# Values of a gated recurrence: products for three heads at a time instead of two

## The chip, the cores and the metric

The kernel runs on one core of a Trainium2 chip. The metric is the time of one execution on the device in microseconds (us). Engines are called as the profile calls them: PE (TensorE, matrix products), DVE (VectorE), ACT (ScalarE), POOL (GpSimd) and SP (SyncE, which here issues most of the DMAs). Matrix products are written to PSUM, in banks of 512 float32 columns; everything else lies in SBUF with 128 partitions.

## The reference

One layer of a decoder on 1024 positions of width 1024: a token mixer with residual, then an MLP with squared ReLU and residual, then a final norm. The mixer makes one projection of the normed input and cuts it into a pooling part (256 columns) and four parts of 768 columns for six heads of a gated linear recurrence. What matters here is where the values `v` come from and who reads them:

```python
h = rms_norm(x, norm_mix_g[l])
u = h @ w_in[l]
u_pool, q_raw, f_raw, i_raw, g_raw = jnp.split(u, splits, axis=-1)
...
k = (1.0 - lbf) * jax.nn.sigmoid(-z)          # z = f_raw; forget f = lb + (1-lb) sigmoid(z)
q = jax.nn.silu(q_raw.astype(jnp.float32))
v = i_raw.astype(jnp.float32)
...
o = (jnp.einsum('bhts,bhsv->bhtv', scores, vb)
     + jnp.einsum('bhtk,bhkv->bhtv', qb * jnp.exp(b), state))
new_state = (jnp.exp(b_last[:, :, 0, :])[..., None] * state
             + jnp.einsum('bhsk,bhsv->bhkv', kb * jnp.exp(b_last - b), vb))
```

Each head has 128 columns of values, so `v` is the product of h (1024 x 1024) with 768 columns of `w_in`, 128 for each head. The outputs of the heads are normed, gated with `silu(g_raw)`, joined with the pooling part and multiplied with `w_out`.

## The kernel before

**Products.** A float32 product is made of three reduced ones: each operand is split into a high part (a cast on ACT) and a low part (a subtraction on DVE), `split` at line 116, and `mm3` at line 121 adds high x high, high x low and low x high. The input lies transposed in `hT`: two halves of 512 positions, each with 8 k-tiles (KT = 8). The row scale of the RMS norm is applied after the products (`rms_col`, `rms_row`, from `row_scales`, line 286).

Queries, forget gates and output gates of a head are "dense_T" products (line 347): 128 columns of weights stand in the array and 512 positions stream through. Each has two halves of 8 steps, and a step is one `mm3` of 512 columns. Values are made the other way round, with positions as the stationary side and weight columns streaming, two heads (a pair, 256 columns) at a time.

**Weights** come through two rings: `raw`, two places for what a DMA brings, and `whi`/`wlo`, four places each for the split parts (`load_w`, line 156). A place is taken again when all readers of its former tile are done. A pair's value weights are two tiles of 4 k-tiles each (`v_weights`, line 214). Values of a head lie in a tile `V`, a ring of three buffers (line 315).

**The start** (lines 643 to 723) has the order of PE, DVE and ACT written out by hand. x arrives k-tile by k-tile with the value weights of the first pair in between; `first_V` (line 268) makes the products of a half of the positions, 96 matmuls, while they arrive. Then come the first halves of q and f of head 0, the second half of x, the second half of the values, the second halves of q and f.

**The heads** (lines 725 to 741) have PE's order written out by hand, while DVE, ACT and POOL are ordered by a planner. A head (`hgrn`, line 394) is a chain of stages, `near`, `middle`, `far`, `keys`, `updates`, `output`; each stage ends in PE work that needs DVE's and ACT's work of the stage before. In front of each stage, PE does a set number of steps of other work, `beside(hd)` (line 602): the q, f and gate products of the next heads and the values of the next pairs. `LAGS` (line 34) holds these numbers: with 48 steps beside a head (the first and the last) 5, 14, 8, 4, 1, 9; with 64 steps 6, 19, 10, 4, 1, 10; head 0 gets 9 more before `near` (`FIRST_LAG`). What is left of `beside` is done after the last stage. Half of a pair's values is made at the end of heads 1 and 3, the other half at the start of heads 2 and 4 (`half_V`, line 595).

The stage `near` starts with two products of q and k, q times the decay, one combining step on q and k (lines 399 to 406, all on DVE) and two copies on ACT (lines 411 and 412); k and the decay come from `forget` (line 365): eviction of the product (line 356, DVE), two sigmoids and a scaling on ACT (368 to 370), and on POOL the decay (371).

After the mixer come `w_out`, the norm, and the MLP, which the change does not touch.

Of the kernel before, what the change touches and what calls it, by code (L numbers as in the profile page):

```python
# [10 lines left out]
F32 = mybir.dt.float32  # L11
F32R = mybir.dt.float32r
# [5 lines left out]
P = 128  # L18
S = 1024
# [13 lines left out]
STAGES = ("near", "middle", "far", "keys", "updates", "output")  # L33
LAGS = {48: dict(zip(STAGES, (5, 14, 8, 4, 1, 9))), 64: dict(zip(STAGES, (6, 19, 10, 4, 1, 10)))}
FIRST_LAG = 9
WARM_UP = 8
MIX_ORDER = (2, 3, 4, 5, 6, 0, 1, 7)
LEVELS = (1, 2, 4, 8, 16, 32)

FIRST_ORDER = (1, 2, 5, 6, 3, 7, 4)  # L40
# [22 lines left out]
def kernel(  # L63
# [116 lines left out]
    with ExitStack() as pa:  # L180
# [32 lines left out]

        def v_weights(pair):
            c0 = V0 + pair * 256
            return [load_w(w_in_v[:, 4 * b:4 * b + 4, c0:c0 + 256], [4, 256], f"v{pair}_{b}") for b in range(2)]

        warm = small.tile([P, 1], F32, tag="ss", name="warm")
        act.activation(warm, nhalf[:, :1], AF.Square)
        act.dma_start(g1, norm_mix_g)  # L220
        act.dma_start(lbl, hgrn_lb_logits)

# [44 lines left out]

        def first_V(h, ws):


            banks = [misc_ps(f"ps_v0_{h}_{i}") for i in range(2)]
            for j in range(KT):
                (wh, wl), b = ws[j // 4], j % 4
                for parts in (((0, wh), (0, wl)), ((1, wh),)):
                    for i in range(4):
                        for part, w in parts:
                            pe.matmul(
                                banks[i // 2][:, i % 2 * 256:(i % 2 + 1) * 256],
                                hT[h][part][:, j, i * P:(i + 1) * P], w[:, b, :],
                                start=j == 0 and i % 2 == 0 and part == 0 and w is wh,  # L280
                                stop=j == KT - 1 and part == 1, skip_group_check=i % 2 == 1,
                            )
                yield
            return banks

        def row_scales(h, tiles):

            ss = small.tile([P, 4], F32, tag="sso", name=f"ssx_{h}")
            for i, t in enumerate(tiles):
                squares = ha.tile([P, D], BF16, tag="pair", name=f"squares_{h}_{i}", bufs=3)  # L290
                act.activation(squares, t, AF.Square, accum_out=ss[:, i:i + 1])
# [4 lines left out]
            pool.tensor_tensor(out=r, in0=ms, in1=nhalf[:, :4], op=ALU.pow)  # L296
# [3 lines left out]
            pt = misc_ps(f"pt_rms_{h}")  # L300
# [11 lines left out]

        def values(pair):
            for hd in (2 * pair, 2 * pair + 1):
                vts[hd] = ha.tile([P, NT, P], F32, tag="V", name=f"V_{hd}", bufs=3)

        def dense_V(pair, ws, i):

            if i == 0:
                values(pair)  # L320
            ps = dense_ps(f"ps_v{pair}_{i}")
            for e in range(2):
                h, c = hT[(i + e) // 4], ((i + e) % 4) * P
                for j in range(KT):
                    w = ws[j // 4]
                    mm3(
                        ps[:, e * 256:(e + 1) * 256],
                        (h[0][:, j, c:c + P], h[1][:, j, c:c + P]),
                        (w[0][:, j % 4, :], w[1][:, j % 4, :]),
                        j == 0, j == KT - 1,  # L330
                    )
                    if j % 2:
                        yield
            return ps

        def scaled_V(pair, ps, i):
            for hd in range(2):
                for e in range(2):
                    act.activation(
                        vts[2 * pair + hd][:, i + e, :], ps[:, e * 256 + hd * P:e * 256 + (hd + 1) * P],  # L340
                        AF.Copy, scale=rms_col[:, i + e:i + e + 1],
                    )

# [233 lines left out]
        def pool_output(kt, u):  # L577
            t = ha.tile([P, S], F32, tag="V", name=f"mix_{kt}", bufs=3)
# [15 lines left out]

        def half_V(pair, half):
            if half == 0:
                pair_w[pair] = v_weights(pair)
            for i in (4 * half, 4 * half + 2):
                ps = yield from dense_V(pair, pair_w[pair], i)
                scaled_V(pair, ps, i)  # L600

        def beside(hd):

            if hd in (2, 4):
                yield from half_V(hd // 2, 1)
            if hd + 1 < NH:
# [7 lines left out]
            if hd + 2 < NH:  # L614
                yield from gate(hd)
            elif hd + 1 < NH:
                pooled[0] = yield from pool_input(0, [mix_tile(NH - 1, f"win{n}_0") for n in range(2)])
            else:
# [8 lines left out]
                yield from work  # L627
            if hd in (1, 3):
                yield from half_V((hd + 1) // 2, 0)

        heads, gates, pair_w, pooled, ready_w, xts, w0 = {}, {}, {}, {}, {}, {}, []

# [10 lines left out]
        with tc.manual_schedule(engines={mybir.EngineType.PE, mybir.EngineType.DVE, mybir.EngineType.Activation}):  # L643
            for j in load_xt(0, (("Q", 2), ("Q", 2), ("K", 2), ("K", 2))):
                xt_hi(0, j)
                if j % 4 == 0:
                    raw = wraw.tile([P, 4, 256], F32, tag="raw", name=f"raw_v0_{j // 4}")
                    w0.append([wring["split"][0].tile([P, 4, 256], F32R, tag=f"w{part}", name=f"w{part}_v0_{j // 4}") for part in ("hi", "lo")])

                n = 1 if j < 2 else 2 if j % 2 == 0 else 0  # L650
                if n:
                    ks = slice(j % 4, j % 4 + n)
                    nc.sync.dma_start(raw[:, ks], w_in_v[:, j:j + n, V0:V0 + 256])
# [5 lines left out]
            xns += [load_rows(i) for i in range(2, 4)]  # L659
            for _ in load_xt(1, (("F", 1), ("V", 3), ("G", 1), ("S", 1))):  # L660
                pass
            xns += [load_rows(i) for i in range(4, NT)]
            split(*later.pop(0))

# [17 lines left out]
            steps(scales, 3)  # L682
            vps = finish(first_V(0, w0))
            work_q, work_f = gated(q, wq, 0, "q_0"), forget(f, k, wf, 0, 0)
            steps(work_q)
            steps(work_f)
            for j in range(KT):
                xt_hi(1, j)
                xt_lo(1, j)
                if j % 2 and j < 4:  # L690
                    scaled_V(0, vps[j // 2], j - 1)
                elif j == 5:
                    finish(scales)
            vps = finish(first_V(1, w0))
            finish(work_q)
            finish(work_f)

# [6 lines left out]
            act.copy(dmask, mraw[:, 2 * len(LEVELS), :])  # L704
            scales = row_scales(1, xns[4:])
            steps(scales, 5)
            for e, ps in enumerate(vps):
                scaled_V(0, ps, 4 + 2 * e)
            ready_w["q"] = q_weights(1)
            work_q = gated(q, wq, 1, "q_0")  # L710
            steps(work_q)
            finish(scales)
            finish(work_q)
# [604 lines left out]
```

## Time and profile before

| | |
|---|---|
| time, median of 3 runs | 1074.33 us (1074.18 to 1074.35) |
| the profiled execution | 1074.34 us, of which 1072.4 us from its first to its last instruction (the span) |
| granted clock of PE | 0.998 |
| PE busy from 4.8 to 29.5 us, the start | 24.33 of 24.70 us |
| PE, DVE, ACT busy from 61.9 to 364.9 us, the six heads | 303.0, 195.9, 150.6 of 303.0 us |
| first product of values | 4.81 us |
| first `near` product of heads 0 to 5 | 61.9, 98.9, 153.7, 208.1, 262.9, 316.6 us |

A line of the chain of waits gives a start, a duration and what ran; "x96" means that so many pieces were merged. A line of the timeline has start, duration, engine, source line, operation, what it writes and reads, and shape; in brackets stands how long the engine sat idle before it and what ended that. A line of a group of instructions ends with busy time, mean of one in ns, and idle time before them with the releaser. Busy times of matmuls overlap; their pace is read from their starts. The rows of stretches (from:to) give length, then busy time and number of instructions for PE, PEld, DVE, ACT and POOL, granted clock, DMA share and GB/s.

### The profile page before, as it was taken

The page shows a single profiled execution, that of the slowest core. Times are in us where ns is not written, and L with a number is a line of the kernel's source. Part 1 is how long each engine was busy: PE and PEld are TensorE (multiplying, and loading weights), DVE is VectorE, ACT ScalarE, POOL GpSimd, SP SyncE. Part 2 cuts the span into 40 slices and gives each one's busy share as a digit, 9 for nine tenths or more (in the row PEclk, how much of TensorE's full clock was granted, in tenths as well). Part 3 has the DMA queues.
Part 4 walks back from the last instruction along what each step waited for, and adds up shares of the span by engine and source line. Part 5 has one row for each costly group of instructions (what it writes and reads, how often), then busy time and mean ns, then how long its engine had stood idle before and what let it go on. Part 6 is the DMA issues. An engine that isn't in the chain of part 4 may idle for free.

```text
span 1072.4 us, 14951 instructions
## 1 busy us (share of the span) xinstructions
PE 1063.8 (99%) x6118; PEld 892.3 (83%) x6118; DVE 740.8 (69%) x922; ACT 446.6 (42%) x716; POOL 79.9 (7%) x125
## 2 busy tenths in 40 slices
PE   9999999999999999999999999999999999999997
PEld 7978898889888788888888888888888888888886
DVE  5488735764576823799856855876879878677775
ACT  7765444554434622473223223323425242423334
POOL 1010000100010111101001101100100000000001
PEclk9999999999999999999999999999999999999999
DMA  9421102110210444135434534428993244254104
GB/s 325 141 77 40 41 21 60 40 41 21 60 40 21 134 142 137 69 108 177 156 116 179 184 100 168 177 96 307 380 348 125 101 174 163 112 197 156 40 1 157
DMA packets 71540, 137.59 MB, mean 128 GB/s; under 512 B 5040, under 2 KB 45104, under 8 KB 67888
## 3 DMA queue, kind: packets, MB, share of 16 engines
q1 hardware_dynamic: 60688, 100.97, 27.8%
q0 software_dynamic: 9344, 33.56, 8.1%
q10 hardware_dynamic: 1440, 2.10, 0.5%
q8 instruction: 48, 0.79, 0.3%
q14 instruction: 20, 0.16, 0.1%
HBM read 98.87 MB, written 37.75 MB: 127 GB/s over the span
## 4 chain that ended last, share of the span: by engine, by line
PE 98%; DMA 0%; DVE 0%; ACT 0%; SPq 0%; issue 0%; POOL 0%; ACTq 0%
PE ps_ua L126 5%; PE ps_ua L125 5%; PE ps_ua L124 5%; PE ps_dx L124 5%; PE ps_dx L125 5%; PE ps_dx L126 5%; PE ps_o L126 3%; PE ps_o L124 3%; PE ps_o L125 3%; PE ps_uc L126 3%; PE ps_dy L124 3%; PE ps_uc L125 3%; PE ps_dy L125 3%; PE ps_dy L126 3%; PE ps_uc L124 3%; PE ps_f L124 2%
## 5 line engine op out<-in xcount | busy, mean ns | idle before, releaser
L118 ACT CAST wdop<-raw_wd 128x2048 fp32r<-128x2048 f32 x28 | 53.6, 1913 | 154.6 <-PE ps_dy L126 49.6
L124 PE MATMUL ps_ua<-h2op,whi_wu 128*128 128x512 f32 x256 | 99.8, 390 | 0.0
L126 PE MATMUL ps_ua<-h2op,wlo_wu 128*128 128x512 f32 x256 | 99.7, 389 | 0.0
L125 PE MATMUL ps_ua<-h2op,whi_wu 128*128 128x512 f32 x256 | 99.7, 389 | 0.0
L126 PE MATMUL ps_dx<-wdop,hop 128*128 128x512 f32 x252 | 98.1, 389 | 0.0
L124 PE MATMUL ps_dx<-wdop,hop 128*128 128x512 f32 x252 | 98.1, 389 | 0.0
L125 PE MATMUL ps_dx<-wdop,hop 128*128 128x512 f32 x252 | 98.1, 389 | 0.0
L119 DVE TENSOR_TENSOR wdop<-raw_wd,wdop 128x2048 fp32r<-128x2048 f32 x28 | 64.1, 2290 | 27.7 <-ACT wdop L118 27.7
L118 ACT CAST hop<-hraw 128x2048 fp32r<-128x2048 f32 x28 | 53.4, 1910 | 33.2 <-DMA hraw<-hid 21.4
L119 DVE TENSOR_TENSOR hop<-hraw,hop 128x2048 fp32r<-128x2048 f32 x28 | 64.0, 2284 | 3.0 <-ACT hop L118 3.0
L118 ACT CAST whi_wu<-wsum 128x1024 fp32r<-128x1024 f32 x22 | 23.2, 1054 | 93.2 <-PE ps_ub L126 27.5
L119 DVE TENSOR_TENSOR wlo_wu<-raw_wu,whi_wu 128x1024 fp32r<-128x1024 f32 x23 | 28.0, 1222 | 47.5 <-ACT whi_wu L118 47.5
L801 DVE TENSOR_TENSOR x<-ps_dx,x 128x512 f32<-128x512 f32 x64 | 43.9, 688 | 18.7 <-PE ps_dx L126 18.7
L125 PEld LDWEIGHTS ps_ua<-h2op,whi_wu 128*128 128x128 f32 x256 | 48.1, 188 | 10.0
L124 PEld LDWEIGHTS ps_ua<-h2op,whi_wu 128*128 128x128 f32 x256 | 48.1, 188 | 10.0
L126 PEld LDWEIGHTS ps_ua<-h2op,wlo_wu 128*128 128x128 f32 x256 | 48.1, 188 | 9.9
L126 PEld LDWEIGHTS ps_dx<-wdop,hop 128*128 128x128 f32 x252 | 47.3, 188 | 9.9
L124 PEld LDWEIGHTS ps_dx<-wdop,hop 128*128 128x128 f32 x252 | 47.3, 188 | 9.8
L125 PEld LDWEIGHTS ps_dx<-wdop,hop 128*128 128x128 f32 x252 | 47.3, 188 | 9.7
L1034 POOL DMA_DIRECT2D hid<-hid x56 | 29.8, 532 | 283.5 <-DVE hid L1031 216.5
L126 PE MATMUL ps_uc<-h2op,wlo_wu 128*128 128x512 f32 x128 | 49.8, 389 | 0.0
L125 PE MATMUL ps_dy<-wdop,hop 128*128 128x512 f32 x128 | 49.8, 389 | 0.0
(271 smaller groups left out, 2771.2 us busy)
## 6 DMA issues: line engine op xcount, KB each, us to landing
hid<-hid POOLq DMA_DIRECT2D x56, 512.0 KB, 3.3
hraw<-hid SPq DMA_DIRECT2D x28, 1024.0 KB, 5.3
raw_wu<-in_w_up_dram SPq DMA_DIRECT2D x32, 512.0 KB, 3.7
raw_wd<-in_w_down_dram SPq DMA_DIRECT2D x16, 1024.0 KB, 7.2
xt<-in_x_t_dram SPq DMA_DIRECT2D x16, 256.0 KB, 5.9
xn<-in_x_dram SPq DMA_DIRECT2D x8, 512.0 KB, 7.5
x<-x_mid SPq DMA_DIRECT2D x8, 512.0 KB, 5.6
raw_q<-in_w_in_dram SPq DMA_DIRECT2D x6, 512.0 KB, 4.0
```

Source lines behind the costliest of these rows:

```text
L118: act.copy(hi, src)
L119: dve.tensor_tensor(out=lo, in0=src, in1=hi.bitcast(F32), op=ALU.subtract)
L124: pe.matmul(ps, lh, rh, start=start, stop=False, skip_group_check=goes_on)
L125: pe.matmul(ps, lh, rl, start=False, stop=False, skip_group_check=goes_on)
L126: pe.matmul(ps, ll, rh, start=False, stop=stop, skip_group_check=goes_on)
L801: dve.tensor_tensor(out=out_, in0=a, in1=b, op=ALU.add)
L1034: nc.gpsimd.dma_start(store[n][:, at, :], t)
```

## The change

Values are made for three heads (384 columns) in one product instead of two (256). There are two trios in place of three pairs:

- The first trio is made ahead of all else: both halves of `first_V`, then everything of q and f of head 0. Four banks hold four row tiles of 384 columns each, three of them from the dense pool (first half) or the misc pool (second half), one from the score pool.
- The second trio is made beside head 2 (`TRIO - 1`), at the start of its side work, 8 row tiles of 8 steps; a step is one `mm3` of 384 columns. Gate 2 is made at the start of the side work of head 3.
- A trio's weights are four tiles of 2 k-tiles each, so they fill the split ring.
- The ring of values has four buffers.
- Heads 1 and 4 have 48 steps beside them and take the lags of 48; head 2 has 96 and a new row of lags; head 3 has 64.
- At the start, all of the second half of x is loaded before any rows, the logits' DMA moves from ACT's queue to SP's behind the first four rows of x, and the second half of x is cast before the norm's squares.

```diff
-LAGS = {48: dict(zip(STAGES, (5, 14, 8, 4, 1, 9))), 64: dict(zip(STAGES, (6, 19, 10, 4, 1, 10)))}
+LAGS = {48: (5, 14, 8, 4, 1, 9), 64: (6, 19, 10, 4, 1, 10), 96: (8, 26, 14, 7, 2, 14)}
+LAGS = {steps: dict(zip(STAGES, lags)) for steps, lags in LAGS.items()}
...
+TRIO = 3
...
-        def v_weights(pair):
-            c0 = V0 + pair * 256
-            return [load_w(w_in_v[:, 4 * b:4 * b + 4, c0:c0 + 256], [4, 256], f"v{pair}_{b}") for b in range(2)]
+        VC = TRIO * P
+
+        def v_weights(trio):
+            c0 = V0 + trio * VC
+            return [load_w(w_in_v[:, 2 * b:2 * b + 2, c0:c0 + VC], [2, VC], f"v{trio}_{b}") for b in range(KT // 2)]
...
-        act.dma_start(lbl, hgrn_lb_logits)
...
-        def first_V(h, ws):
-
-
-            banks = [misc_ps(f"ps_v0_{h}_{i}") for i in range(2)]
+        def first_V(h, ws, place):
+
+
+            banks = [(score_ps if i == 3 else place)(f"ps_v0_{h}_{i}") for i in range(4)]
             for j in range(KT):
-                (wh, wl), b = ws[j // 4], j % 4
+                (wh, wl), b = ws[j // 2], j % 2
                 for parts in (((0, wh), (0, wl)), ((1, wh),)):
                     for i in range(4):
                         for part, w in parts:
                             pe.matmul(
-                                banks[i // 2][:, i % 2 * 256:(i % 2 + 1) * 256],
-                                hT[h][part][:, j, i * P:(i + 1) * P], w[:, b, :],
-                                start=j == 0 and i % 2 == 0 and part == 0 and w is wh,
-                                stop=j == KT - 1 and part == 1, skip_group_check=i % 2 == 1,
+                                banks[i][:, :VC], hT[h][part][:, j, i * P:(i + 1) * P], w[:, b, :],
+                                start=j == 0 and part == 0 and w is wh, stop=j == KT - 1 and part == 1,
                             )
...
+        def values(trio):
+            for hd in range(TRIO * trio, TRIO * (trio + 1)):
+                vts[hd] = ha.tile([P, NT, P], F32, tag="V", name=f"V_{hd}", bufs=4)
+
+        def dense_V(trio):
+
+            ws = v_weights(trio)
+            values(trio)
+            for i in range(NT):
+                h, c = hT[i // 4], i % 4 * P
+                ps = dense_ps(f"ps_v{trio}_{i}")
                 for j in range(KT):
-                    w = ws[j // 4]
+                    w = ws[j // 2]
                     mm3(
-                        ps[:, e * 256:(e + 1) * 256],
-                        (h[0][:, j, c:c + P], h[1][:, j, c:c + P]),
-                        (w[0][:, j % 4, :], w[1][:, j % 4, :]),
+                        ps[:, :VC], (h[0][:, j, c:c + P], h[1][:, j, c:c + P]), (w[0][:, j % 2, :], w[1][:, j % 2, :]),
                         j == 0, j == KT - 1,
                     )
-                    if j % 2:
-                        yield
-            return ps
+                    yield
+                scaled_V(trio, ps, i)
...
         def beside(hd):
 
-            if hd in (2, 4):
-                yield from half_V(hd // 2, 1)
+            if hd == TRIO - 1:
+                yield from dense_V(1)
+            elif hd == TRIO:
+                yield from gate(hd - 1)
...
             if hd + 2 < NH:
-                yield from gate(hd)
+                if hd != TRIO - 1:
+                    yield from gate(hd)
...
-            if hd in (1, 3):
-                yield from half_V((hd + 1) // 2, 0)
...
-                if j % 4 == 0:
-                    raw = wraw.tile([P, 4, 256], F32, tag="raw", name=f"raw_v0_{j // 4}")
...
+                if j % 2 == 0:
+                    raw = wraw.tile([P, 2, VC], F32, tag="raw", name=f"raw_v0_{j // 2}")
...
+            for _ in load_xt(1, (("F", 1), ("V", 4), ("G", 1), ("S", 1))):
+                pass
+            xns = [load_rows(i) for i in range(4)]
+            nc.sync.dma_start(lbl, hgrn_lb_logits)
             wq = q_weights(0, early_raw("T", "q_0"), put_off)
-            xns = [load_rows(i) for i in range(2)]
             wf = f_weights(0, early_raw("Kn", "f0"), put_off)
...
+            vps = finish(first_V(0, w0, dense_ps))
+            for j in range(KT):
+                xt_hi(1, j)
+                xt_lo(1, j)
...
-            scales = row_scales(0, xns[:4])
-            steps(scales, 2)
+            scales = [row_scales(0, xns[:4], dense_ps), row_scales(1, xns[4:])]
+            steps(scales[0], 5)
             split(*later.pop(0))
...
+            for i, ps in enumerate(vps):
+                scaled_V(0, ps, i)
+            vps = finish(first_V(1, w0, misc_ps))
+            split(*later.pop(0))
+            steps(scales[1], 5)
+            finish(scales[0])
+            for i, ps in enumerate(vps):
+                scaled_V(0, ps, 4 + i)
...
             ready_w["q"] = q_weights(1)
-            work_q = gated(q, wq, 1, "q_0")
-            steps(work_q)
-            finish(scales)
-            finish(work_q)
+            finish(gated(q, wq, 0, "q_0"))
             ready_w["f"] = f_weights(1)
+            finish(forget(f, k, wf, 0, 0))
+            finish(scales[1])
+            finish(gated(q, wq, 1, "q_0"))
             finish(forget(f, k, wf, 1, 0))
...
-                lags = LAGS[64 if 0 < hd < NH - 1 else 48]
+                lags = LAGS[{TRIO - 1: 96, TRIO: 64}.get(hd, 48)]
```

More of the change, by code (lines that the diff above doesn't have):

```diff
@@ L284, in first_V, with row_scales @@
             return banks
-        def row_scales(h, tiles):
+        def row_scales(h, tiles, place=misc_ps):
             ss = small.tile([P, 4], F32, tag="sso", name=f"ssx_{h}")
@@ L299, in row_scales @@
             yield
-            pt = misc_ps(f"pt_rms_{h}")
+            pt = place(f"pt_rms_{h}")
             for i in range(4):
@@ L311, in finish, with scaled_V @@
                     return end.value
[L313 to L323, printed above, removed]
+        def values(trio):
[7 more added lines that the diff above has]
+                ps = dense_ps(f"ps_v{trio}_{i}")
                 for j in range(KT):
-                    w = ws[j // 4]
+                    w = ws[j // 2]
                     mm3(
-                        ps[:, e * 256:(e + 1) * 256],
-                        (h[0][:, j, c:c + P], h[1][:, j, c:c + P]),
-                        (w[0][:, j % 4, :], w[1][:, j % 4, :]),
+                        ps[:, :VC], (h[0][:, j, c:c + P], h[1][:, j, c:c + P]), (w[0][:, j % 2, :], w[1][:, j % 2, :]),
                         j == 0, j == KT - 1,
                     )
-                    if j % 2:
-                        yield
-            return ps
[L336 to L342, printed above, removed]
+                    yield
+                scaled_V(trio, ps, i)
+        def scaled_V(trio, ps, i):
+            for n in range(TRIO):
+                act.activation(
+                    vts[TRIO * trio + n][:, i, :], ps[:, n * P:(n + 1) * P], AF.Copy, scale=rms_col[:, i:i + 1]
+                )
         def col_tile(c0, name, raw=None, parts=split):
@@ L577, in pool_output @@
         def pool_output(kt, u):
-            t = ha.tile([P, S], F32, tag="V", name=f"mix_{kt}", bufs=3)
+            t = ha.tile([P, S], F32, tag="V", name=f"mix_{kt}", bufs=4)
             for b in range(2):
@@ L593, in gate @@
                 yield from gated(g, wg, h, f"g_{hd}")
[L595 to L600, printed above, removed]
         def beside(hd):
-            if hd in (2, 4):
-                yield from half_V(hd // 2, 1)
+            if hd == TRIO - 1:
+                yield from dense_V(1)
+            elif hd == TRIO:
+                yield from gate(hd - 1)
             if hd + 1 < NH:
@@ L627, in beside @@
                 yield from work
-            if hd in (1, 3):
-                yield from half_V((hd + 1) // 2, 0)
-        heads, gates, pair_w, pooled, ready_w, xts, w0 = {}, {}, {}, {}, {}, {}, []
+        heads, gates, pooled, ready_w, xts, w0 = {}, {}, {}, {}, {}, []
         def steps(work, n=KT):
@@ L645 @@
                 xt_hi(0, j)
-                if j % 4 == 0:
-                    raw = wraw.tile([P, 4, 256], F32, tag="raw", name=f"raw_v0_{j // 4}")
-                    w0.append([wring["split"][0].tile([P, 4, 256], F32R, tag=f"w{part}", name=f"w{part}_v0_{j // 4}") for part in ("hi", "lo")])
+                if j % 2 == 0:
+                    raw = wraw.tile([P, 2, VC], F32, tag="raw", name=f"raw_v0_{j // 2}")
+                    w0.append([wring["split"][0].tile([P, 2, VC], F32R, tag=f"w{part}", name=f"w{part}_v0_{j // 2}") for part in ("hi", "lo")])
                 n = 1 if j < 2 else 2 if j % 2 == 0 else 0
                 if n:
-                    ks = slice(j % 4, j % 4 + n)
-                    nc.sync.dma_start(raw[:, ks], w_in_v[:, j:j + n, V0:V0 + 256])
+                    ks = slice(j % 2, j % 2 + n)
+                    nc.sync.dma_start(raw[:, ks], w_in_v[:, j:j + n, V0:V0 + VC])
                     split(w0[-1][0][:, ks], w0[-1][1][:, ks], raw[:, ks])
                 xt_lo(0, j)
+            for _ in load_xt(1, (("F", 1), ("V", 4), ("G", 1), ("S", 1))):
+                pass
+            xns = [load_rows(i) for i in range(4)]
+            nc.sync.dma_start(lbl, hgrn_lb_logits)
             wq = q_weights(0, early_raw("T", "q_0"), put_off)
-            xns = [load_rows(i) for i in range(2)]
             wf = f_weights(0, early_raw("Kn", "f0"), put_off)
-            xns += [load_rows(i) for i in range(2, 4)]
-            for _ in load_xt(1, (("F", 1), ("V", 3), ("G", 1), ("S", 1))):
-                pass
             xns += [load_rows(i) for i in range(4, NT)]
-            split(*later.pop(0))
+            vps = finish(first_V(0, w0, dense_ps))
+            for j in range(KT):
+                xt_hi(1, j)
+                xt_lo(1, j)
             mx = small.tile([P, NH], F32, tag="lbt", name="lb_shift")
@@ L678 @@
             values(0)
-            scales = row_scales(0, xns[:4])
-            steps(scales, 2)
+            scales = [row_scales(0, xns[:4], dense_ps), row_scales(1, xns[4:])]
+            steps(scales[0], 5)
             split(*later.pop(0))
-            steps(scales, 3)
-            vps = finish(first_V(0, w0))
-            work_q, work_f = gated(q, wq, 0, "q_0"), forget(f, k, wf, 0, 0)
-            steps(work_q)
[L686 to L692, printed above, removed]
-                    finish(scales)
-            vps = finish(first_V(1, w0))
-            finish(work_q)
-            finish(work_f)
+            for i, ps in enumerate(vps):
[6 more added lines that the diff above has]
+                scaled_V(0, ps, 4 + i)
             pool.memset(ones, 1.0)
```

7 lines of the change are left out of this document (removed).

## The prediction

> **What bounds the kernel now.** I read the page first (busy shares and rate of loading), then TensorE's list of waits, then the chain of waits.
>
> ```profile
> span 1072.4 us, 14951 instructions
> PE 1063.8 (99%) x6118; PEld 892.3 (83%) x6118; DVE 740.8 (69%) x922; ACT 446.6 (42%) x716; POOL 79.9 (7%) x125
> ...
> GB/s 325 141 77 40 41 21 60 40 41 21 60 40 21 134 142 137 69 108 177 156 116 179 184 100 168 177 96 307 380 348 125 101 174 163 112 197 156 40 1 157
> ```
>
> ```profile
> PE warm L225 <- DVE junk L223: 1.2, 1, 1.2
> PE ps_v L277 <- DVE wlo_v L119: 0.3, 1, 0.3
> ```
>
> TensorE (PE) is busy for 99% of the span, and its waits in all are 1.5 us, both at the start. In the six heads it never waits. So an edit counts in two ways only: by how much time the matmuls take end to end, and by any wait that it puts in front of TensorE. Work on VectorE (DVE), ScalarE (ACT) or the queues is free until it makes TensorE wait.
>
> What does a matmul cost in a stream? Busy times overlap, so I take starts from the chain: 96 products of 256 columns in one piece, and, from a stretch of the MLP, 24 products of 512 columns between two starts.
>
> ```profile
> 29.53 11.51 PE ps_v L277 x96
> ```
>
> ```profile
> 504.97 0.23 PE ps_ua L124
> ...
> 510.41 0.23 PE ps_uc L124
> ```
>
> 11.51/96 = 119.9 ns for 256 columns; 5.44/24 = 226.7 ns for 512. The difference is 106.8 ns for 256 columns, or 0.417 ns a column, which leaves 13.1 ns that every matmul pays whatever its width. For 384 columns, an estimate by the same line: 13.1 + 160.2 = 173.3 ns.
>
> **Part 1: fewer, wider products.** Before, values take 3 pairs x 8 row tiles x 8 k-tiles x 3 terms = 576 matmuls of 256 columns, 576 x 0.1199 = 69.06 us. After, 2 trios x 8 x 8 x 3 = 384 of 384 columns, 66.55 us. The saving is 192 fixed shares of 13.1 ns, 2.5 us.
>
> [...]
>
> **Part 2: the start.** The first value weights arrive with the first x tiles, and now each k-tile brings half as many bytes again.
>
> ```profile
> 3.05 4.93 DMA raw_v<-in_w_in_dram
> 8.00 0.63 ACT whi_v L118
> 8.65 0.70 DVE wlo_v L119
> 9.40 8.79 PE ps_v L277 x71
> ```
>
> ```profile
> 52.69 1.05 ACT L118 CAST whi_g<-raw_g 128x1024 fp32r<-128x1024 f32 x1 [2.01 <-DMA raw_g<-in_w_in_dram]
> ```
>
> ```profile
> 53.77 1.22 DVE L119 TENSOR_TENSOR wlo_g<-raw_g,whi_g 128x1024 fp32r<-128x1024 f32 x1 [0.60 <-ACT whi_g L118]
> ```
>
> Today the weights of k-tiles 2 and 3 land at 7.98 us; after a cast and a subtraction TensorE starts the second product of k-tile 2 at 9.40, and 71 of the half's 96 products remain. The 25 products before that hide inside the loading. After, 262 KB more have to land by then (half of 524 KB); at the page's 325 GB/s that is 0.8 us. The two splits work on 768 instead of 512 columns: between 0.63 and 1.05 for the cast, so 0.84; between 0.70 and 1.22 for the subtraction, so 0.96. So 9.40 becomes 9.40 + 0.8 + 0.21 + 0.26, about 10.6 us. From there it is matmuls alone: before 9.40 + (71 + 96 + 384) x 0.1199 = 75.5; after 10.6 + (71 + 96 + 192) x 0.1733 = 72.8. **Parts 1 and 2 together: -2.6 us.** Bounds: the 25 wider products take 4.33 us themselves, and they start at about 4.9, so 9.8 is the earliest with a few at the slow pace of the start (-3.4); weights another 0.8 us late give -1.8.
>
> What else is moved at the start. The raw ring has two places, so the weights of k-tiles 4-5 and 6-7 are issued on SP only after the split of tiles 0-1 and 2-3, and x tiles 5 to 7, the second half of x, all rows, the logits (which leave ACT's queue for SP's) and the raw q and f stand behind them on SP. A k-tile now occupies TensorE for 12 x 0.1733 = 2.1 us, so k-tile 6 is needed at about 18.8 us; its weights, issued at 10.6 and in transit for the 4.93 us of the row above, are split by about 17.3. All four places of the split ring hold first-trio weights; the split of q therefore waits on ACT until TensorE has done k-tile 1 of the second half, and the scaling of the values and the other squares queue behind it. The cover is the second half itself, 96 x 0.1733 = 16.6 us.
>
> ```profile
> L339 ACT ACTIVATE V<-ps_v,rms_col 128x128 f32<-128x128 f32 x48 | 14.2, 372 | 17.1 <-PE ps_v L126 15.4 <-POOL rms_col L296 1.5
> L291 ACT ACTIVATE squares<-xn 128x1024 bf16<-128x1024 f32 x8 | 8.4, 1047 | 0.4 <-DMA xn<-in_x_dram 0.2
> ```
>
> ACT has 8 squares (8.4), 12 scalings (at most 12 x 0.37 = 4.4) and two casts (2.1) to do there, 14.9 us. They begin when the logits land, behind 7.9 MB, which at 325 GB/s is some 25 us from the start, and end at about 40; the first result of TensorE that needs them, the row scales for the first q product, is due at about 45 (10.6 + 167 x 0.1733 + 24 x 0.2267). I cost it at nothing; without that cover it would be up to 3 us.
>
> **Part 3: the third head, where a wait appears.** Work beside head 2 now ends with the forget product of head 3, because gate 2 has moved to the front of head 3's own side work. The first scores of head 3 ("near") follow only 6 steps later. What they need is a chain: evict the forget product, two sigmoids and a scaling on ACT (the decay factor is made on POOL beside them), then five passes on DVE, then two copies on ACT. Head 0 shows this chain in today's trace, since there too the forget product comes last, but with 14 steps (5 + 9) in front. First TensorE, then DVE, then ACT:
>
> ```profile
> 52.28 0.39 PE L124 MATMUL ps_q<-hT_hi,whi_q 128*128 128x512 f32 x1
> ```
>
> ```profile
> 52.48 0.69 DVE L356 TENSOR_TENSOR K<-ps_f,rms_row 128x512 f32<-128x512 f32 x1 [0.54 <-PE ps_f L126]
> ...
> 55.73 1.23 DVE L399 TENSOR_TENSOR d<-Q,K 128x1024 f32<-128x1024 f32 x1 [0.74 <-ACT K L370]
> 57.06 1.23 DVE L400 TENSOR_TENSOR Q<-Q,F 128x1024 f32<-128x1024 f32 x1
> 58.21 1.22 DVE L119 TENSOR_TENSOR wlo_q<-raw_q,whi_q 128x1024 fp32r<-128x1024 f32 x1
> 59.34 0.69 DVE L402 TENSOR_TENSOR d<-Q,K 128x512 f32<-128x512 f32 x1
> 59.94 0.68 DVE L356 TENSOR_TENSOR Q<-ps_q,rms_row 128x512 f32<-128x512 f32 x1
> 60.54 0.68 DVE L531 TENSOR_TENSOR Q<-Q,F 128x512 f32<-128x512 f32 x1
> 61.14 0.69 DVE L532 TENSOR_TENSOR K<-K,F 128x512 f32<-128x512 f32 x1
> ```
>
> ```profile
> 53.65 0.63 ACT L368 ACTIVATE F<-K 128x512 f32<-128x512 f32 x1
> 54.31 0.63 ACT L369 ACTIVATE K<-K 128x512 f32<-128x512 f32 x1
> 54.97 0.73 ACT L370 ACTIVATE K<-K,om 128x512 f32<-128x512 f32 x1
> ...
> 61.26 0.66 ACT L411 COPY kq<-Q 128x512 f32<-128x512 f32 x1
> 61.92 0.70 ACT L412 COPY kq<-K 128x512 f32<-128x512 f32 x1
> ```
>
> ```profile
> 61.96 0.79 PE sc_near L392 x16
> 62.75 0.39 PE sc_near L420 x32
> ```
>
> TensorE left the forget product at 52.28 and the last copy ended at 62.62, 10.34 us later; near's last products came 0.05 us after that. Two operations on DVE were not of the chain: the split of other weights (58.21 to 59.34, 1.13) and a q eviction (59.94 to 60.54, 0.60). Without them near's last products could start 10.39 - 1.73 = 8.7 us after the forget product. After the change TensorE has 6 steps x 3 x 0.2267 = 4.1 us, some 0.1 for the switch, and 0.8 us of column sums (61.96 to 62.75) before it needs those copies: 5.0 us. **It waits 8.7 - 5.0 = 3.7 us**, in pieces: first for d, then for the second d, then for the copies. Bounds: the cast at 52.69 held the first sigmoid back by about 0.4, so 3.3 without it, 3.0 if another pass overlaps; with both strangers of head 0, 5.4. I take 3.7: the q eviction can't come in (TensorE has finished no later product by then), and the ring place that a second split would need is still held by gate 2. Today head 3 has no such wait, since gate 2 and half a pair of values stand in between:
>
> ```profile
> 189.79 0.23 PE ps_g L124
> ...
> 208.15 0.79 PE sc_near L392 x16
> ```
>
> The forget product of head 3 is left at 189.79, near comes at 208.15, 18.4 us for the same 8.7.
>
> **Part 4: heads 1 and 4 lose side work** (11.5 us each) and take the short lags of 48 steps. Heads 0 and 5 have these lags today and show no wait, so nothing is the likeliest price.
>
> ```profile
> 61.90:98.90 37.00, 37.00 (x352) 30.70 (x355) 30.69 (x62) 22.57 (x52) 4.36 (x4) 1.00 0.17 49
> 98.90:153.70 54.80, 54.80 (x498) 48.75 (x498) 30.81 (x57) 24.63 (x59) 4.06 (x4) 1.00 0.11 30
> ```
>
> In the window of head 0 DVE (third busy column) is busy 30.69 of 37.0 us; head 1 has 30.81 of 54.8, so about 31 of 43.3 after. Before the second trio starts, its last weights wait for gate 1's ring place; cast and subtraction (0.84 + 0.96 and 0.2 of hand-over) take 2.0 us, and TensorE asks for them after 6 steps of 0.52 us, 3.1. At its end the split of q for head 3 takes 0.2 + 1.05 + 1.22 = 2.5 against the same 3.1. Zero for both; up to 1.5 us for all of part 4 if DVE is taken when they come. The fourth value buffer removes no wait that the trace shows: zero.
>
> **Sum**, against the profiled execution, 1074.34 us (0.01 above the median of 1074.33, and 1.94 outside the span): 1074.34 - 2.6 + 3.7 = **1075.4 us**. A measurement here can tell 0.2%, 2.15 us, from no change, so "same" is 1072.2 to 1076.5. The case's own range, from -3.4 + 3.0 to -1.8 + 4.1, is 1073.9 to 1076.6.
>
> **Rivals.** *A, no wait at head 3*: the merged product brings its 2.6 us, 1071.7. For it: today's TensorE waits nowhere in the heads. Against: the d pass at 55.73 reads all 1024 columns of k, which exist only after the last scaling, and 8.7 us of passes don't fit into 5.0. *B, the wait takes the long form of head 0*: strangers get between the passes on DVE, near's last products come 10.4 us after the forget product, TensorE waits 5.4: 1077.1. It decides slower as soon as the wait exceeds 2.15 + 2.6 = 4.75 us, about one split of 1.13 more than I count. For it: head 0 shows both; against: the ring and eviction reasons above. *C, part 4 isn't free*: 1.5 us on top of my sum, 1076.9, from the short lags or the two ring hand-overs, DVE being at 83% in head 0. *D, the clock*: the array's first products start 0.22 us apart (5.65 to 5.87), where the piece of 96 above has 0.120, and the slow stretch ran from the first matmul at 1.2 us to about 6.1. If the waits of part 3 bring such a stretch back, half of its 4.9 us is lost, 2.4 more: 1077.8.
>
> ```profile
> 5.65 0.41 PE L277 MATMUL ps_v<-whi_v,hT_hi 128*128 128x256 f32 x1
> 5.87 0.41 PE L277 MATMUL ps_v<-wlo_v,hT_hi 128*128 128x256 f32 x1
> ...
> 8.68 0.39 PE L277 MATMUL ps_v<-whi_v,hT_hi 128*128 128x256 f32 x1
> 9.40 0.39 PE L277 MATMUL ps_v<-wlo_v,hT_hi 128*128 128x256 f32 x1 [0.34 <-DVE wlo_v L119]
> ```
>
> Against D: the pause from 8.68 to 9.40 was followed by products at full pace, and mine are pieces of about that kind. [...]
>
> **Chances.** Forecast 0.56, A 0.14, B 0.17, C 0.08, D 0.05. Faster is A, 0.14; slower is B, C and D, 0.30; same 0.56. The range must reach A on one side and B on the other: 1071.5 to 1078.0, which leaves out two mishaps at once.
>
> **What would show it.** Products of 384 columns start 173 ns apart, the second product of k-tile 2 starts near 10.6 us, and TensorE's list of waits has sc_near waiting for DVE and ACT at one head, 3 to 4 us in all, with clock 1.00 throughout. Near of head 3 without a wait refutes part 3; waits at heads 1 or 4, or on the weights of the trio, refute part 4; 176 ns or more refutes part 1.

## The result, and the profile after

| | before | after |
|---|---|---|
| median | 1074.26 us (1073.84 to 1074.35, 4 runs) | 1086.13 us (1084.8 to 1086.33, 4 runs) |
| ratio | | 1.0109, 95% interval 1.0091 to 1.0126 |
| the profiled execution, its span | 1074.34, 1072.4 us | 1085.95, 1084.2 us |
| granted clock | 0.998 | 0.993 |
| first `near` product of heads 0 to 5 | (above) | 71.7, 107.8, 151.7, 218.3, 277.9, 321.0 us |
| first `w_out` product, first MLP product | 359.8, 454.9 us | 369.3, 466.6 us |

The change costs 11.9 us. The forecast was 1075.4, its range 1071.5 to 1078.0: wrong, on the slower side of everything that it had.

First the page of the changed kernel, then its list of waits of PE (engine, line and tile, what ended the wait: us in total, times, longest):

```profile
span 1084.2 us, 14577 instructions
PE 1066.9 (98%) x5926; PEld 893.9 (82%) x5926; DVE 738.4 (68%) x922; ACT 445.9 (41%) x716; POOL 78.3 (7%) x125
...
PEclk9999999989999899999999999999999999999999
```

```profile
PE ps_o L127 <- DVE g L360: 5.0, 1, 5.0
PE sc_near L417 <- ACT kq L409: 1.7, 1, 1.7
PE sc_near L389 <- DVE d L399: 1.4, 1, 1.4
PE warm L229 <- DVE junk L227: 1.2, 1, 1.2
PE sc_near L389 <- DVE d L396: 1.1, 1, 1.1
```

Three short waits of `sc_near` are the ones that were forecast. One wait of 5.0 us is new: `w_out`'s first product (`ps_o`) waits for the multiplication of an output gate (`g`, line 360) with which it shares no data. And the row of the granted clock (PEclk, in tenths of full speed) has two 8s, in the slices with these two places in them, where the kernel before has 9s throughout:

```profile
PEclk9999999999999999999999999999999999999999
```

In the table of stretches (from:to, length, then busy time and instructions of PE, PEld, DVE, ACT, POOL, granted clock, DMA share, GB/s) the two places stand out:

```profile
223.07:228.36 5.29, 5.29 (x19) 4.15 (x13) 5.24 (x12) 3.71 (x7) 0.00 (x0) 0.50 0.02 5
...
364.38:369.34 4.96, 0.00 (x1) 0.00 (x0) 4.96 (x9) 3.73 (x7) 0.00 (x0) 0.92 0.22 89
369.34:375.43 6.09, 6.09 (x15) 4.79 (x15) 4.16 (x7) 1.38 (x3) 0.00 (x0) 0.51 0.80 272
```

In the first and last of them PE is "busy" all the time, at half the clock. The pace shows it in single products: PE's timeline of the changed kernel around `near` of head 3.

```profile
216.84 0.39 PE L129 MATMUL ps_g<-hT_hi,wlo_g 128*128 128x512 f32 x1
218.29 0.64 PE L389 MATMUL sc_near<-d,ones 128*32 128x256 f32 x8 [1.06 <-DVE d L396]
220.37 0.43 PE L389 MATMUL sc_near<-d,ones 128*32 128x128 f32 x8 [1.44 <-DVE d L399]
222.49 0.66 PE L417 MATMUL sc_near<-kq 128*32 128x32 f32 x32 [1.69 <-ACT kq L409]
223.07 0.80 PE L127 MATMUL ps_g<-hT_hi,whi_g 128*128 128x512 f32 x1
...
224.09 0.63 PE L129 MATMUL ps_g<-hT_hi,wlo_g 128*128 128x512 f32 x1
224.52 0.63 PE L127 MATMUL ps_g<-hT_hi,whi_g 128*128 128x512 f32 x1
...
228.36 0.50 PE L127 MATMUL ps_g<-hT_hi,whi_g 128*128 128x512 f32 x1
```

The starts behind the waits lie 0.43 us apart (224.09, 224.52) where before had 0.227. From 223.07 to 228.36 stand 12 products, 5.29 us where 12 x 0.227 = 2.72 would do: some 2.6 us lost. Behind the wait of `ps_o` 14 products take the 6.09 us of the row above instead of 3.17: 2.9 lost.

**Where the time went.** By the first `w_out` product the changed kernel is 369.34 - 359.82 = 9.5 us behind: values and start -2.8 (below), the waits before `near` 1.06 + 1.44 + 1.69 = 4.2, half pace behind them 2.6, the wait before `w_out` 5.0, and 0.5 that is left over, about what `near`'s own products take more when the waits cut them apart (0.64 + 0.43 + 0.66 = 1.7 us against the 0.79 + 0.39 = 1.2 of before). From there to the first MLP product it takes 97.3 us instead of 95.0, 2.3 of the 2.9 lost to half pace, since four gaps between products that before has some 10 us behind `w_out`'s first product, 0.6 us in all, are gone there. The rest of the kernel takes 617.6 us in both. 9.5 + 2.3 = 11.8, as the spans have it.

**The wait before `w_out`.** DVE's timeline over the wait, first of the changed kernel, then of the kernel before:

```profile
363.86 2.49 DVE L122 TENSOR_TENSOR mT_lo<-mix,mT_hi 128x512 fp32r<-128x512 f32 x4
366.26 0.69 DVE L353 TENSOR_TENSOR g<-ps_g,rms_row 128x512 f32<-128x512 f32 x1
366.87 0.69 DVE L122 TENSOR_TENSOR mT_lo<-mix,mT_hi 128x512 fp32r<-128x512 f32 x1
367.46 1.22 DVE L122 TENSOR_TENSOR wlo_wo<-raw_wo,whi_wo 128x1024 fp32r<-128x1024 f32 x1
368.60 0.69 DVE L360 TENSOR_TENSOR g<-ps_g,g 128x512 f32<-128x512 f32 x1
```

```profile
361.87 0.69 DVE L356 TENSOR_TENSOR g<-ps_g,rms_row 128x512 f32<-128x512 f32 x1
...
364.20 0.69 DVE L363 TENSOR_TENSOR g<-ps_g,g 128x512 f32<-128x512 f32 x1
```

The gate's eviction and its multiplication stand equally far apart, 2.34 us after the change and 2.33 before. Before, too, the last gate was finished late (364.20 + 0.69 = 364.89, 5.1 us after `w_out`'s first product at 359.82), and nobody waited for it. After, `w_out` starts only when it is done (368.60 + 0.69 = 369.29; 369.34). So the work did not get slower; a tie was added. The suspect is the PSUM bank: the gate's product lies in PSUM until that multiplication has read it.

The dense pool gives its three banks out in turn. Before, `first_V` and the row scales (`pt_rms_0`) took none of them. After, the first half of the first trio takes three and `pt_rms_0`, which the diff moves there from the misc pool, takes one: four tiles, one more than a full turn, so every later dense tile lies one place further round. In the compiled kernels the second half of the last gate lies in bank 1 before and in bank 0 after; `w_out`'s first tile lies in bank 0 in both.

### The profile page after: what moved, and what is told of

Same layout as the page of the kernel before. It is cut to its first block, busy times and chain, and to the rows that moved or that the text cites. A ratio compares the mean times of both kernels' runs of the same rounds, so it can differ in the third digit from the quotient of the medians.

```text
span 1084.2 us, 14577 instructions
## 1 busy us (share of the span) xinstructions
PE 1066.9 (98%) x5926; PEld 893.9 (82%) x5926; DVE 738.4 (68%) x922; ACT 445.9 (41%) x716; POOL 78.3 (7%) x125
## 4 chain that ended last, share of the span: by engine, by line
PE 96%; DVE 2%; ACT 0%; POOL 0%; issue 0%; ACTq 0%; POOLq 0%
PE ps_ua L127 5%; PE ps_ua L129 5%; PE ps_ua L128 5%; PE ps_dx L128 5%; PE ps_dx L129 5%; PE ps_dx L127 5%; PE ps_v L281 3%; PE ps_o L127 3%; PE ps_o L128 3%; PE ps_o L129 3%; PE ps_dy L128 3%; PE ps_uc L127 3%; PE ps_uc L129 3%; PE ps_dy L129 3%; PE ps_dy L127 3%; PE ps_uc L128 3%
## 5 line engine op out<-in xcount | busy, mean ns | idle before, releaser
L127 PE MATMUL ps_uc<-h2op,whi_wu 128*128 128x512 f32 x128 | 49.9, 390 | 0.0
```

What stands on the lines that cost most here:

```text
L127: pe.matmul(ps, lh, rh, start=start, stop=False, skip_group_check=goes_on)
```

## The experiments

Theory T: three things make the loss: the wait before `near` of head 3 (DVE's and ACT's chain), the bank that `w_out` has to wait for, and half pace behind each wait because PE stood idle. Rival R1: one cause, such as a transfer or the planner's order, makes both waits. Rival R2: the half pace belongs to the work behind the waits and not to the idle time. The runs came in three groups. In each the kernel before ran beside them, with medians of 1074.42, 1074.77 and again 1074.42 us, and the ratios below are taken against these.

**The lag alone.** Head 3 gets the 9 further steps before `near` that head 0 has.

```diff
-for _ in range(lags[stage] + (FIRST_LAG if hd == 0 and stage == "near" else 0)):
+for _ in range(lags[stage] + (FIRST_LAG if hd in (0, TRIO) and stage == "near" else 0)):
```

> The kernel after, with 9 more steps of side work before near of head 3 (15 in place of 6). My theory: the loss of 11.9 us is made of -2.8 (values), +4.2 (three waits before near of head 3), +2.4 (array at half pace for some 5 us behind them), +5.1 (the first product of w_out waits for the bank of the last gate) and +2.8 (half pace behind that). Here the second and third go: 1086.1 - 6.6 = 1079.5, no sc_near in the list of waits, and no products 0.427 us apart behind near. Rival: DVE and ACT are late in head 3 as a whole, and the wait moves to its next stage: within 1 us of 1086.1.

Measured 1078.27 us (1078.25 to 1078.79), ratio 1.0036 (1.0023 to 1.0049). The waits of `sc_near` are gone, `ps_o`'s 5.0 us remains. Against R1: the two waits come apart.

**The bank alone.** The row scales of the first half go through a score bank; nothing else moves.

```diff
-scales = [row_scales(0, xns[:4], dense_ps), row_scales(1, xns[4:])]
+scales = [row_scales(0, xns[:4], score_ps), row_scales(1, xns[4:])]
```

> The kernel after, with the transposed row scales of the first half in a bank of the score pool instead of one of the dense pool. That is one dense tile fewer, so that the last gate product ends in another bank than the first product of w_out takes. My theory: the wait of 5.0 us before ps_o and the half pace behind it go, while the waits of 0.4 that the kernel before has there come back: 1086.1 - 5.1 - 2.8 + 0.4 = 1078.6. Rival: DVE is late at the end of head 5, and the first product of w_out waits for it whatever bank it has: within 1 us of 1086.1.

Measured 1078.09 us (1077.08 to 1079.0), ratio 1.0033 (1.0021 to 1.0045). One word in the start, over 300 us ahead, removes the wait before `w_out`, 8.0 us off the 1086.13. The last gate is finished as late as ever (367.18 + 0.69 = 367.87, 5.1 us after `w_out`'s first product at 362.79), but nobody waits for it. The three waits of `sc_near` stay as they were, 1.7, 1.4 and 1.1 us.

**The bank in the kernel before.** One product near the end of the heads takes a dense bank instead of a score bank, so that the turn is shifted without anything of the change.

```diff
-ps = score_ps(f"psp_{kt}_{b}")
+ps = (dense_ps if (kt, b) == (0, 0) else score_ps)(f"psp_{kt}_{b}")
```

> The kernel before, with the first product of the first pooling output in a bank of the dense pool instead of the score pool: one dense tile more, so that the last gate product ends in the bank that the first product of w_out takes. Nothing of the trios is in it. My theory (the bank decides): 1074.3 + 4.7 + 2.8 = 1081.8, with ps_o waiting for g on DVE for about 5 us. Rival (the trios make DVE late): 1074.3, no wait.

Measured 1081.27 us (1080.48 to 1081.8), ratio 1.0062 (1.0047 to 1.0077). PE's list of waits of this run, whose lines are numbered as in the kernel before, has the changed kernel's entry:

```profile
PE ps_o L124 <- DVE g L363: 5.0, 1, 5.0
```

The kernel before loses 6.9 us by the shift alone. The place of a tile in the turn is the cause of this wait.

**Work instead of idle time before `near`.** Sixteen further products keep PE at work while the chain of head 3 runs.

```diff
+if stage == "near" and hd == TRIO:
+    for n in range(2):
+        fill = score_ps(f"fill_{n}")
+        for _ in range(8):
+            pe.matmul(fill, hT[0][0][:, 0, :P], hT[0][0][:, 0, :], start=True, stop=True)
```

> The kernel after, with 16 products more (512 columns of the input, into score banks that nobody reads) just before near of head 3, about 3.6 us of work that computes nothing needed. My theory: near starts when its inputs are there, as before, but the array does not idle, so the products behind it keep their pace of 0.227 us: 1086.1 - 2.4 = 1083.7. Rival: the half pace has another cause than idleness (the inputs, or DVE and PE on the same memory): 1086.1, products behind near 0.427 us apart. If the filling only delays near: up to 1089.

Measured 1083.19 us (1082.68 to 1083.7), ratio 1.0082 (1.0065 to 1.0099). The chain takes as long as before, the last `near` products start at 222.50 (222.49 without the fill), but what follows runs at full pace. PE's timeline of this run:

```profile
222.50 0.46 PE L417 MATMUL sc_near<-kq 128*32 128x32 f32 x32 [0.82 <-ACT kq L409]
222.88 0.50 PE L127 MATMUL ps_g<-hT_hi,whi_g 128*128 128x512 f32 x1
...
224.15 0.39 PE L129 MATMUL ps_g<-hT_hi,wlo_g 128*128 128x512 f32 x1
224.38 0.39 PE L127 MATMUL ps_g<-hT_hi,whi_g 128*128 128x512 f32 x1
```

The same products as in the changed kernel, 0.23 us apart where that had 0.43, and the granted clock is 1.00 from 222.88 to 228.00. Against R2, and 2.9 us gained by useless work.

**Both edits together** (the lag and the bank).

> The kernel after with both edits: 9 more steps before near of head 3, and the row scales' transposes in a score bank. My theory: the two losses are independent, each with its own wait and its own stretch at half pace, so both go, and what is left is the gain of the wider products and of the start. From the two single runs 1086.1 - 7.9 - 8.0 = 1070.2; from the terms before - 2.8 = 1071.5. No wait of TensorE but that at the very start. Rival: one loss hides the other or a third wait comes up behind: 1074 or more.

Measured 1071.66 us (1071.44 to 1071.86), ratio 0.997 (0.9958 to 0.9981). PE's waits are those of the start alone:

```profile
PE warm L229 <- DVE junk L227: 1.2, 1, 1.2
PE ps_v L281 <- DVE wlo_v L122: 0.2, 1, 0.2
```

What is left is what the wider products bring: 3.1 us by the medians, 2.7 by the spans (1069.7 against 1072.4). The savings of the two single runs, 7.9 and 8.0 us, would have added up to 1070.2; 1.5 us of that did not come. This fits stretches of half pace whose length differs from run to run (see what stays open), but it is not shown to be that alone.

**Gate 2 back behind head 2's other work, and the bank.** The cause of the short lead is undone where it arose: the 16 steps of gate 2 stand between the forget product and `near` again.

```diff
-            elif hd == TRIO:
-                yield from gate(hd - 1)
...
-                if hd != TRIO - 1:
-                    yield from gate(hd)
+                yield from gate(hd)
...
-lags = LAGS[{TRIO - 1: 96, TRIO: 64}.get(hd, 48)]
+lags = LAGS[{TRIO - 1: 96}.get(hd, 48)]
```

> The kernel after with gate 2 moved back to the end of the work beside head 2 (lags of 48 for head 3, those of 96 for head 2), and the row scales' transposes in a score bank; near of head 3 keeps few steps (5). My theory: near's wait comes from the forget product standing last, not from the number of lag steps as such: with 16 steps of gate 2 behind the forget product no sc_near wait, 1070 to 1072, as with the longer lag. Rival (five steps are too few by themselves, or gate 2's place matters for something else): a wait before near of head 3 of 2 us or more, 1074 or more.

Measured 1071.41 us (1071.21 to 1071.45), ratio 0.9967 (0.9954 to 0.998): the best of all, faster than both kernels. PE's list of waits has no `sc_near`, though only 5 steps are set in front of `near`: what had made it wait was the forget product standing last.

**Half the lag, and the bank.** Four further steps before `near` of head 3 instead of nine.

> As the run with both edits, but 4 more steps before near of head 3 instead of 9, that is 2.7 us of the some 4.4 that were missing. Waits before near of 1.7 us in all remain. My theory: an idle time this short leaves the array's pace as it is, so the run is 1.7 us above that with both edits, and products behind near stay 0.227 us apart. Rival: any wait before near slows the array behind it: 3 to 4 us above.

Measured 1073.99 us (1073.29 to 1075.81, 11 runs), ratio 0.9995 (0.9986 to 1.0004), 2.3 above the full lag instead of 1.7. Its times form two groups: six from 1073.3 to 1074.0, 1.6 to 2.3 above the full lag, and five from 1075.0 to 1075.8. The profiled execution, 1073.29, is of the first, and its table of stretches and its waits have 2.0 us of waits and no half pace:

```profile
PE sc_near L417 <- ACT kq L409: 1.7, 1, 1.7
PE warm L229 <- DVE junk L227: 1.2, 1, 1.2
PE sc_near L389 <- DVE d L399: 0.3, 1, 0.3
```

```profile
223.01:228.00 4.99, 4.99 (x32) 4.12 (x23) 4.95 (x12) 3.81 (x6) 0.00 (x0) 1.00 0.00 2
```

No trace was kept of the second group, but each execution's mean granted clock is on record: 0.998 in all six of the first group, 0.997 in all five of the second. So the half pace coming back in some executions fits both the size and the clock; how long and where it lasted in them is not shown.

**Work instead of idle time before `w_out`.** The kernel with the lag alone, with 22 or with 11 further products between the heads and `w_out`.

```diff
+fill = score_ps("fill")
+for _ in range(22):
+    pe.matmul(fill, hT[0][0][:, 0, :P], hT[0][0][:, 0, :], start=True, stop=True)
```

> The changed kernel with the longer lag before near of head 3 (that variant: 1078.27 us, w_out's first product waits 5.0 us for gate 5's multiplication, and some 13 products behind the wait start 0.427 us apart instead of 0.227). Here 22 further products of 512 columns (22 x 0.227 = 5.0 us) into a score bank that nothing reads are put between the heads and w_out, so that TensorE works through the wait. If the half pace comes from TensorE standing idle, it is gone with the idle time: 1078.27 - 13 x 0.2 = 1075.7, up to 0.3 more where the fill ends behind the wait. If the half pace belongs to w_out's start (its weights or splits being late) and not to the idleness, it stays: 1078.3. If gate 5's multiplication is itself pushed later by the fill, 1079 or more.

With 11, where the half pace is what may come back:

> The same with 11 further products (2.5 us), so that 2.5 us of idle time are left of 5.0, in one piece. [...] If idle time of 2.5 us can bring it back, as the wait of 2.0 us before near of head 3 with the half lag seems to do in some executions, the time lies between 1075.7 and 1078.3 and moves from one execution to the next by up to 2 us.

Measured: with 22, 1076.03 us (1075.56 to 1076.99), ratio 1.0017 (1.0007 to 1.0027); with 11, 1074.30 us (1073.78 to 1074.42), ratio 0.9997 (0.9987 to 1.0007). The first is 2.2 us below the lag alone. PE's timeline of it:

```profile
357.49 5.15 PE L728 MATMUL fill<-hT_hi 128*128 128x512 f32 x22
362.47 0.39 PE L127 MATMUL ps_o<-whi_wo,mT_hi 128*128 128x512 f32 x1
362.70 0.39 PE L128 MATMUL ps_o<-wlo_wo,mT_hi 128*128 128x512 f32 x1
```

5.0 us of work stand where the lag alone has 5.0 us of waiting, and behind them the pace is full: starts 0.23 us apart, where the run with the lag alone has a granted clock of 0.50 from 362.06 to 367.00. As for the transfers: behind the wait of the changed kernel the granted clock was 0.51 at a DMA share of 0.80, but the kernel before has 1.00 at a share of 0.99 from 6.24 to 8.02 us, with full pace (products of 256 columns start 0.12 us apart). So busy DMA engines alone do not halve the pace.

The run with 11 missed its expectation, on the good side: 1.4 us below the lower end, and within 0.64 us from one execution to the next. Its DVE timeline and PE's waits tell why:

```profile
357.34 0.69 DVE L122 TENSOR_TENSOR mT_lo<-mix,mT_hi 128x512 fp32r<-128x512 f32 x1 [0.86 <-PE ps_g L128]
357.95 0.69 DVE L353 TENSOR_TENSOR g<-ps_g,rms_row 128x512 f32<-128x512 f32 x1
...
359.68 0.69 DVE L360 TENSOR_TENSOR g<-ps_g,g 128x512 f32<-128x512 f32 x1
```

```profile
PE warm L229 <- DVE junk L227: 1.2, 1, 1.2
PE ps_o L127 <- DVE g L360: 0.4, 1, 0.4
PE ps_v L281 <- DVE wlo_v L122: 0.2, 1, 0.2
```

With the further products in PE's order the planner put the gate's eviction ahead of the splits of the mixed tiles (`mT_lo`): one of them stands in front of it, not four, and none between it and the multiplication. The gate was done some 3 us after PE could have gone on, not 5.0. So the size of the bank wait was the planner's order on DVE, and the run says nothing on 2.5 us of idle time, since only 0.4 was left. The run with 22 has the same order on DVE: its gate was done at 360.49 (359.80 + 0.69), 2.0 us before the 22 products ended, so some 9 of them were more than the bank asked for. What that run shows of the pace holds all the same, since PE did not stand still.

## Why the prediction was wrong, point by point

**Part 1, fewer and wider products: right.** 173.3 ns was forecast for 384 columns. PE's timeline of the changed kernel has 128x384 products at these starts (30.30 stands for four):

```profile
29.95 0.33 PE L281 MATMUL ps_v<-whi_v,hT_hi 128*128 128x384 f32 x1
30.13 0.33 PE L281 MATMUL ps_v<-wlo_v,hT_hi 128*128 128x384 f32 x1
30.30 0.85 PE L281 MATMUL ps_v<-whi_v,hT_lo 128*128 128x384 f32 x4
30.99 0.33 PE L281 MATMUL ps_v<-whi_v,hT_hi 128*128 128x384 f32 x1
31.17 0.33 PE L281 MATMUL ps_v<-wlo_v,hT_hi 128*128 128x384 f32 x1
```

(31.17 - 29.95)/7 = 174 ns; the median of all steps from one such product to the next is 173. So the line through two widths, with its fixed 13 ns a product, holds at a third. The whole of values, summed over the starts, fell from 71.4 to 68.6 us: -2.8 against -2.6.

**Part 2, the start: about right in its number, in part by luck.** The second product of k-tile 2 was forecast at 10.6 us and started at 10.27, between the forecast and its bound of 9.8. The forecast made it wait for later weights; but PE's list of waits has none for them. The 25 wider products in front of it set the time: they took 5.5 us from 4.77 on, the first five at 0.28 to 0.59 us each. Neither the moved DMAs nor ACT's queue made PE wait. But this is also where the step that failed lies. The part followed the queues, the split ring and ACT, and not the banks: it put four more tiles in the dense pool, one of them the row scales, at nothing without a word.

**Part 3, the wait before `near` of head 3: right mechanism, mis-sized by 0.5.** 3.7 us in three pieces, first for d, then for the second d, then for the copies, was forecast; 4.2 came, in those pieces, between the bounds of 3.0 and 5.4 that the part worked out, but just above the 4.1 with which the case's own range was added up, a figure that stands nowhere in the working. What was short is the chain: 9.5 us from the first gate product behind the forget product (212.99) to `near`'s last products (222.49), not 8.7; PE's own work in that time was 5.3 us, not 5.0. The strangers on DVE were not the two of head 0 but the passes that make powers of the decay (`dec`):

```profile
215.95 0.69 DVE L532 TENSOR_TENSOR dec<-F 128x512 f32<-128x512 f32 x1 [0.68 <-POOL F L368]
216.68 0.42 DVE L532 TENSOR_TENSOR dec<-dec 128x256 f32<-128x256 f32 x1
217.02 1.22 DVE L396 TENSOR_TENSOR d<-Q,K 128x1024 f32<-128x1024 f32 x1
```

k was ready when ACT's scaling ended at 215.97 (215.25 + 0.72); d began at 217.02. That is 1.05 us lost to two passes that nobody was waiting for yet; three smaller ones follow between the other passes. On the other side, the cast that held head 0's first sigmoid back by 0.4 us cost 0.04 here (it ran from 212.96; K's eviction ended at 213.88, the sigmoid began at 213.92).

**Rival D, the clock: named, sized at 2.4, and given 0.05.** It came, twice, with 2.6 at `near` and 2.3 net at `w_out`. What talked it down was the pause from 8.68 to 9.40 us, behind which the pace was full. But in that pause PE stood idle for 0.34 us, far less than the 4.2 to come, and that these came in pieces of at most 1.69, with matmuls between, did not save the pace: the granted clock behind them is 0.50. Behind the 4.96 us in one piece at `w_out` it is 0.51. In one thing these stretches differ from the start's slow one, which was the model for D: there the granted clock is 1.00 from 1.20 to 6.10 us, so that by the traces the two have only their pace in common.

**Rival A, no wait at head 3: refuted as stated,** since the three waits came. It is what the lag and the bank, or gate 2 and the bank, made of the kernel: 1071.7 was its price, 1071.66 and 1071.41 were measured.

**Part 4, heads 1 and 4 and the ring hand-overs: right at nothing.** No wait there, and the short lags hold; the stretch from `near` of head 1 to `near` of head 2 and that of head 4 have PE busy throughout:

```profile
107.80:151.73 43.93, 43.93 (x390) 37.62 (x389) 29.69 (x57) 21.96 (x51) 3.97 (x5) 1.00 0.10 29
...
277.89:321.03 43.14, 43.14 (x380) 36.21 (x379) 29.98 (x58) 21.22 (x49) 4.07 (x4) 1.00 0.11 37
```

**The step that failed** is the sum, by two terms that it put at nothing: the wait for a bank behind the heads, and the half pace behind any wait. It held four parts, all of them in the start and the heads, and took everything behind the heads as unchanged. With -2.8 and 4.2 in the places of -2.6 and 3.7 it would have given 1075.7. The 5.0 us of the bank, the 4.9 us (2.6 + 2.3) of half pace and the 0.5 around `near` were the miss, 10.4 us, and the bank alone would have carried the time out of the range (1075.7 + 5.0 = 1080.7). Within each pool the kernel gives the banks out in turn; the tie arose where one pool's turn ends and another pool takes over its banks, and the run with the bank alone agrees, 5.0 us of wait against none.

**What stays open.** Why the stretch of half pace differs from run to run (5 products behind `near` in the run with the bank alone, with a granted clock of 0.75 from 223.07 to 228.00; 12 in the changed kernel, with 0.50 from 223.07 to 228.36; after the same three waits). By the granted clocks it differs from one execution to the next as well: the profiled one of the run with the bank alone, with its 5, has 0.997 and is the fastest of six; the other five, up to 1079.0 us, have 0.994 to 0.996. And which idle time in one piece just brings it about is not shown: no single wait of these runs lies between 1.7 and 5.0 us.

## What to carry to other kernels

A pool of buffers that is given out in turn has a phase. An edit that takes one buffer more or fewer from it moves every later tile by a place, so besides the new waits at the edit, look at the places where a pool is handed over, and ask which late reader holds the bank that the next stage writes first. Where PE is the bound, count a wait of some us at its length plus the half-pace stretch that may follow it (here 2.9 us behind 5.0 in one piece, and 2.6 behind 4.2 in three pieces); and if a chain must end before PE gets there, give it steps of other work.

## What the runs showed of the hardware

- Three waits of 1.06, 1.44 and 1.69 us within 6 us, with short matmuls between, brought a granted clock of 0.50 for the next 5.29 us in the changed kernel, and 5 products at half pace with the bank alone; a single wait of 0.8 us behind a fill, or of 1.65 and 0.3 us in one execution, brought none (granted clock 1.00 in both).
- A wait of 4.96 us in one piece brought a granted clock of 0.51 for the next 6.09 us. With the lag alone it was 0.50 from 362.06 to 367.00, behind 5.0 us; with 5.0 us of further products in the place of that wait the starts were 0.23 us apart, not 0.43. A DMA share of 0.99, from 6.24 to 8.02 us in the kernel before, went with a granted clock of 1.00 and full pace.
- Products that nobody reads can pay: 16 of them took 2.9 us off the changed kernel, 22 took 2.2 us off the one with the lag alone, and 11 took 4.0 off, there because the planner's order on DVE changed as well.
